# All high products of a chunk's two blocks, then all its low ones, in a two-layer transformer on one core

## The chip, the cores and the metric

The kernel runs on one core of one Trainium2 chip. The metric is the device time of one execution in microseconds; the median of three runs is given. Times of single instructions come from one profiled execution.

## What is computed

Two transformer layers of different kinds follow each other on one sequence of 256 positions with 1024 channels, all in float32. The first joins a gated linear recurrence with a causal attention of 8 heads and a feed-forward part with a causal convolution and GELU; the second joins a windowed attention with a sink and a latent attention, and a SiLU feed-forward part. Most of the work is products of the normed input with weight matrices:

```python
def first_block(x, ...):
    h = rmsnorm(x, norm1_g[l])
    u = jnp.einsum('bsd,de->bse', h, w_in[l])          # recurrence, gates, q, k, v
    ...
    merged = gates0 * (ya @ w_proj_rnn[l]) + gates1 * (yb @ w_proj_attn[l])
    x = x + merged @ w_out[l]
    h = rmsnorm(x, norm2_g[l])
    up = causal_dwconv(h @ w_up[l], ffn_conv_w[l], ffn_conv_b[l])
    x = x + (gelu(up) * (h @ w_gate[l])) @ w_down[l]

def second_block(x, ...):
    proj = rmsnorm_2(x, mix_norm_g[l]) @ w_in[l]
    ...                                                # two attentions of 8 heads
    y = sigmoid(g_a) * (o_a @ w_o_swa[l]) + sigmoid(g_b) * (o_b @ w_o_mla[l])
    x = x + y @ w_out[l]
    h = rmsnorm_2(x, ffn_norm_g[l])
    x = x + (silu(h @ w_gate[l]) * (h @ w_up[l])) @ w_down[l]
    return rmsnorm_2(x, final_norm_g)
```

## The kernel before

The float32 products are made of products in a shorter format (fp32r). A weight chunk of 128 partitions and 2048 columns (1408 in the two down products) comes by one DMA on SP's queue into `wt`; ACT writes its rounded copy `wh`, and DVE the rest, `wl = wt - wh`. Inputs are split in the same way: a tile of `X` holds, for each of two blocks of 128 channels, 256 columns of rounded values and then 256 of the rest. There are three buffers each for `wt`, `wh` and `wl`, and chunks are made two ahead.

A product needs high x high, high x rest and rest x high. For one step k of 128 channels, `group` (L513) issues two matmuls into one PSUM bank of 512 columns. The **high** one takes `wh` as its stationary operand and streams all 512 columns of the input, so that columns 0 to 255 of the bank collect high x high and 256 to 511 collect high x rest. The **low** one takes `wl`, streams the 256 rounded columns and adds into columns 256 to 511. `total` (ACT and DVE) later adds the bank's halves. In `group` high and low of one step stand together: high, low, low, high, low, high and so on.

`mm_T` (L528) makes a chunk of 256 output channels, two blocks b with a bank each, over 8 steps: the first 6 steps of block 0 and of block 1, then the last two of each, since a stage's last input tile may be late. One chunk is 16 highs and 16 lows. It serves `w_x`, `w_g`, the gates, `w_pr`, `w_pa`, `w_out`, `w_up`, `w_gate` and their counterparts of the second layer; `w2_o` uses it in halves of 4 steps. The down products use `group` alone, 11 steps for each chunk (`mm_down` L545, and a loop of its own at the end of the second layer, whose last block goes through `group1` L535, with matmuls of 256 columns only). The projections of the attentions go through `mm_A` (L552), where the weights stream in up to 512 columns and the input is the stationary operand.

What order the instructions stand in is decided by a list scheduler (`Scheduler`). Each instruction has a price in microseconds; the scheduler walks through a modelled time and gives each engine the first instruction in program order that is ready then, or the one that is ready soonest. An instruction waits for those that write what it reads, and for every instruction in `sch.after` at the time it is added. So in the attentions matmuls of `mm_T` stand between the scores, the transposes of the probabilities and the products with the values as fillers. All instructions are issued at L333, which is why every row of the profile has that line.

Of the kernel before, what the change touches and what calls it, by code (L numbers as in the profile page):

```python
# [17 lines left out]
P = 128  # L18
WARM = 4
S = 256  # L20
D = 1024
KD = D // P
# [313 lines left out]
class Engines:  # L336
# [5 lines left out]
    def act(self, out, in_, func, **kw):  # L342
        n = max(out.n, in_.n)
        cost = (0.053 if in_.tile.psum else 0.093) + n / 1200.0
        cost += 0.09 * sum(isinstance(kw.get(k), View) for k in ("scale", "bias")) + (0.1 if "accum_out" in kw else 0.0)
        return self.sch.add("ACT", self.nc.scalar.activation, cost, (out, in_, func), kw, table=SETS.get(func))

    def mm(self, out, a, b, start, stop):
        n = out.n
        if b.dtype == F32R and n >= 256:  # L350
            cost = n / 2400.0 + 0.003
        elif b.dtype == BF16:
            cost = n / 2400.0 + 0.003
        elif n == 1:
            cost = 0.11
        else:
            cost = 4 * n / 2400.0 + 0.006
        self.sch.add("PE", self.nc.tensor.matmul, cost, (out, a, b), dict(start=start, stop=stop, skip_group_check=True))

    def transpose(self, out, in_, idn):  # L360
        self.sch.add("PE", self.nc.tensor.transpose, 2 * out.n / 2400.0 + 0.003, (out, in_, idn), {})
# [28 lines left out]
def build(tc, A, out):  # L390
    from contextlib import ExitStack


    order = []
    _build(None, tc, Scheduler(), A, out, None, order)
    sch = Scheduler()
    with ExitStack() as ctx:
        _build(ctx, tc, sch, A, out, order, [])
        sch.emit(tc)


def _build(ctx, tc, sch, A, out, order, used):
# [19 lines left out]
    mm_ = V.mm  # L422

    def U():
        return up.tile([P, 2, S], F32, tag="u")
# [4 lines left out]
    def T():  # L430
        return tp.tile([P, 2, S], F32, tag="t")
# [10 lines left out]
    def MM():  # L442
        return [B(), B()]
# [29 lines left out]
    def vc(name, i, n=1):  # L473
        return vec[:, VEC[name] + i : VEC[name] + i + n]
# [7 lines left out]
    def produce():  # L482
        i = state["next"]
        name, idx = order[i]
        n = A[name].shape[-1]
        wt = wp.tile([P, 2048], F32, tag="wt")
        wh = wp.tile([P, 2048], F32R, tag="wh")
        wl = wp.tile([P, 2048], F32R, tag="wl")


        cuts = [0, n // 2, n] if i < 4 or i >= fine else [0, n]
        for a, b in zip(cuts, cuts[1:]):
            V.dma("sync", wt[:, a:b], A[name][idx][:, a:b])
            act(wh[:, a:b], wt[:, a:b], AF.Copy)
            V.tensor_sub(wl[:, a:b], wt[:, a:b], wh[:, a:b].bitcast(F32))
        ready[i] = (wh, wl)
        state["next"] = i + 1

    def chunk(name, idx):
        i = len(used)  # L500
        used.append((name, idx))
        if order is None:
            t = wp.tile([P, 2048], F32R, tag="wh")
            return t, t
        assert order[i] == (name, idx)
        while state["next"] <= min(i + LOOK, len(order) - 1):
            produce()
        return ready.pop(i)

    def mv(X, k):  # L510
        return X[k // 2][:, k % 2].rearrange("p h t -> p (h t)")

    def group(ps, W, X, ks, first, last, width, col, xk=0):  # L513

        wh, wl = W
        for k in ks:
            c = slice(k * width + col, k * width + col + P)
            m = mv(X, xk + k)
            hi = lambda st, sp: mm_(ps, wh[:, c], m, start=st, stop=sp)
            lo = lambda: mm_(ps[:, S:], wl[:, c], m[:, :S], start=False, stop=False)  # L520
            if k == first:
                hi(True, False)
                lo()
            else:
                lo()
                hi(False, k == last)

    def mm_T(ps, W, X, kb=KD, k0=0, xk=0):  # L528

        ks = list(range(k0, k0 + kb))  # L530
        for part in (ks[:-2], ks[-2:]):
            for b in range(2):
                group(ps[b], W, X, part, k0, k0 + kb - 1, 256, b * P, xk=xk - k0)

    def group1(ps, W, X, ks, first, last, width, col, xk=0):  # L535

# [29 lines left out]
    def total(ps, dst=None):  # L566

        t = T()
        dst = t if dst is None else dst
        for b in range(2):  # L570
            act(t[:, b], ps[b][:, S:], AF.Copy)
            V.tensor_add(dst[:, b], ps[b][:, :S], t[:, b])
        return dst

    def split(src, X=None):
        X = X or R()
        act(X[:, :, 0], src, AF.Copy)
        V.tensor_sub(X[:, :, 1], src, X[:, :, 0].bitcast(F32))
        return X
# [92 lines left out]
    for k in range(8):  # L672
# [3 lines left out]
        last = V.tensor_sub(w[:, 1], t, w[:, 0].bitcast(F32))  # L676
# [120 lines left out]
    YB = []  # L797
# [50 lines left out]
    def pad():  # L848
        npad[0] += 1
        return pads[npad[0] % 2]  # L850

    YA, HH, XA = [], [], []
# [77 lines left out]
    def gate(name, p, X, later=None):  # L930
        ps = MM()
        mm_T(ps, chunk(name, p), X)
        s = U()
        total(ps, s)
        V.tensor_mul(s, s, rsb)
        if later is None:
            act(s, s, AF.Sigmoid)
        else:
            later.append(s)
        return s  # L940

    M, gates = [], []
    for i in range(6):
        if i < 4:
            gates.append((gate("w_g0", i, X1), gate("w_g1", i, X1)))
        if i < 2:
            continue
        p = i - 2
        g0, g1 = gates[p]
        ps = MM()  # L950
        mm_T(ps, chunk("w_pr", p), YA)
        m0 = total(ps)
        V.tensor_mul(g0, g0, m0)
        ps = MM()
        mm_T(ps, chunk("w_pa", p), YB)
        m1 = total(ps)
        V.tensor_mul(m1, m1, g1)
        V.tensor_add(m1, m1, g0)
        M.append(split(m1))

    def residual(name, X, xin, gname):

        xs, Xs, n = [], [], Norm()
        for p in range(4):
            ps = MM()
            mm_T(ps, chunk(name, p), X)
            y = U()
            for b in range(2):
                V.tensor_add(y[:, b], ps[b][:, :S], xin[p][:, b])
                V.tensor_add(y[:, b], ps[b][:, S:], y[:, b])  # L970
            Xs.append(split_gain(y, gname, p))
            n.add(y)
            xs.append(y)
        return xs, Xs, n

    def down(name, X, xin, rs, gname):
# [12 lines left out]
        return xs, Xs, n  # L989

    x2, X2, n2 = residual("w_out", M, x, "norm2_g")
    rsb = None
    F = []
    for p in range(11):
        ps = MM()
        mm_T(ps, chunk("w_up", p), X2)
        if p == 0:
            rsb, _ = n2.done()
        xr = pad()
        t = total(ps)  # L1000
        V.tensor_mul(xr[:, :, 4:], t, rsb)
        g = T()
        for b in range(2):
            n = 2 * p + b
            act(g[:, b], xr[:, b, 2 : 2 + S], AF.Copy, scale=vc("ffn_conv_w", n))
            for k in range(1, 3):
                V.scalar_tensor_tensor(g[:, b], xr[:, b, 2 + k : 2 + k + S], vc("ffn_conv_w", 22 * k + n), g[:, b], op0=ALU.mult, op1=ALU.add)
            act(g[:, b], g[:, b], AF.Gelu_apprx_tanh, bias=vc("ffn_conv_b", n))
        ps = MM()
        mm_T(ps, chunk("w_gate", p), X2)  # L1010
        t = total(ps)
        V.tensor_mul(t, t, g)
        F.append(split(t))
# [26 lines left out]
    ps = MM()  # L1040
# [19 lines left out]
    ps = MM()  # L1060
# [36 lines left out]
    ps = MM()  # L1097
# [7 lines left out]
    for i in range(2):  # L1105
        pt = B2()
        for hp in range(2):
            for j in range(2):
                c = (2 * i + hp) * P
# [14 lines left out]
    for half in range(2):  # L1124
        ps = MM()
# [38 lines left out]
    for c in range(2):  # L1164
        ps = MM()
# [11 lines left out]
    OS, OM = [], []  # L1177
# [53 lines left out]
    for p in range(4):  # L1231
        W = chunk("w2_o", p)
        ps = MM()
        mm_T(ps, W, OS, kb=4, k0=0)
        m0 = total(ps)
        V.tensor_mul(m0, m0, GA[p])
        ps = MM()
        mm_T(ps, W, OM, kb=4, k0=4)
        m1 = total(ps)
        V.tensor_mul(m1, m1, GB[p])  # L1240
        V.tensor_add(m1, m1, m0)
        Y.append(split(m1))

    x4, X4, n4 = residual("w2_out", Y, x3, "ffn_g")
    F = []
    for p in range(11):
        ps = MM()
        mm_T(ps, chunk("w2_gate", p), X4)
        if p == 0:
            rsb, _ = n4.done()  # L1250
        g = total(ps)
        V.tensor_mul(g, g, rsb)
        silu = act(g, g, AF.Silu)
        V.tensor_mul(g, g, rsb)
        ps = MM()
        mm_T(ps, chunk("w2_up", p), X4)
        t = total(ps)
        V.tensor_mul(t, t, g)
        F.append(split(t))
# [4 lines left out]
    for p in range(4):  # L1264
        y = U()
        ps = MM()
        for b in range(2):
            tail = p == 3 and b == 1
            for j in range(2):
                W = chunk("w2_down", 4 * p + 2 * b + j)  # L1270
# [118 lines left out]
```

## Time and profile before

| | us |
|---|---|
| median of 3 runs | 812.02 |
| lowest, highest | 811.87, 812.77 |
| the profiled execution in all | 812.49 |
| its span, first to last instruction | 810.7 |
| PE busy | 798.5 |
| DVE busy | 603.8 |
| ACT busy | 524.1 |

All busy times are of the profiled execution. In a timeline each line is one instruction, or several of a kind merged, with its start and its duration in us. A matmul begins before the one ahead of it has ended, so durations overlap; what a matmul costs is the distance from its start to that of the next.

### The profile page before, as it was taken

The page shows a single profiled execution, that of the slowest core. Times are in us where ns is not written, and L with a number is a line of the kernel's source. Part 1 is how long each engine was busy: PE and PEld are TensorE (multiplying, and loading weights), DVE is VectorE, ACT ScalarE, POOL GpSimd, SP SyncE. Part 2 cuts the span into 40 slices and gives each one's busy share as a digit, 9 for nine tenths or more (in the row PEclk, how much of TensorE's full clock was granted, in tenths as well). Part 3 has the DMA queues.
Part 4 walks back from the last instruction along what each step waited for, and adds up shares of the span by engine and source line. Part 5 has one row for each costly group of instructions (what it writes and reads, how often), then busy time and mean ns, then how long its engine had stood idle before and what let it go on. Part 6 is the DMA issues. An engine that isn't in the chain of part 4 may idle for free.

```text
span 810.7 us, 11872 instructions
## 1 busy us (share of the span) xinstructions
PE 798.5 (98%) x4520; PEld 689.1 (85%) x4520; DVE 603.8 (74%) x1023; ACT 524.1 (65%) x907; POOL 1.9 (0%) x7
## 2 busy tenths in 40 slices
PE   8999999999999999999999999999999999999996
PEld 6888888888888888888888888888888888888886
DVE  6777869977779788888566776565889877877553
ACT  7979889955455766666445667767656755655451
POOL 0000000000000000000000000000000000000000
PEclk9999999999999999999999999999999999999999
DMA  9742445455555454543556545432456665644541
GB/s 306 308 179 104 163 162 180 158 208 200 171 200 190 174 179 186 207 151 135 193 192 233 187 144 169 144 102 76 134 157 207 204 194 178 204 152 151 179 143 52
DMA packets 32540, 141.05 MB, mean 174 GB/s; under 512 B 3618, under 2 KB 5412, under 8 KB 24420
## 3 DMA queue, kind: packets, MB, share of 16 engines
q1 hardware_dynamic: 32100, 139.41, 50.4%
q0 software_dynamic: 240, 0.79, 0.3%
q8 instruction: 35, 0.57, 0.3%
q14 instruction: 21, 0.17, 0.1%
q10 hardware_dynamic: 144, 0.11, 0.0%
HBM read 139.24 MB, written 1.05 MB: 173 GB/s over the span
## 4 chain that ended last, share of the span: by engine, by line
PE 94%; ACT 2%; DMA 1%; DVE 1%; SPq 0%; issue 0%; DVEq 0%; ACTq 0%
PE b_banks L333 94%; DMA wt_wp<-in_w_q 1%; ACT wh_wp L333 1%; DMA u_up<-in_w_k 1%; ACT t_tp L333 1%; DVE wl_wp L333 0%; SPq L333 0%; DVE u_up L333 0%; DVE t_tp L333 0%; ACT pr_ap L333 0%; DVE pr_ap L333 0%; ACT k_cp L333 0%; DVEq L1384 0%; ACT u_up L333 0%; DVE k_cp L333 0%
## 5 line engine op out<-in xcount | busy, mean ns | idle before, releaser
L333 PE MATMUL b_banks<-r_rp,wh_wp 128*128 128x512 f32 (+1 forms) x1782 | 610.5, 395 | 0.0
L333 PE MATMUL b_banks<-r_rp,wl_wp 128*128 128x256 f32 x1760 | 462.7, 281 | 0.0
L333 PEld LDWEIGHTS b_banks<-r_rp,wh_wp 128*128 128x128 f32 x1782 | 320.6, 188 | 58.8
L333 DVE TENSOR_TENSOR wl_wp<-wt_wp,wh_wp 128x1024 fp32r<-128x1024 f32 (+4 forms) x197 | 299.6, 1537 | 68.2 <-ACT wh_wp L333 67.5
L333 PEld LDWEIGHTS b_banks<-r_rp,wl_wp 128*128 128x128 f32 x1760 | 331.6, 189 | 18.1
L333 ACT ACTIVATE wh_wp<-wt_wp 128x1024 fp32r<-128x1024 f32 (+4 forms) x197 | 253.2, 1308 | 71.0 <-PE b_banks L333 60.3
L333 ACT ACTIVATE t_tp<-b_banks 128x256 f32<-128x256 f32 (+1 forms) x180 | 69.2, 388 | 155.3 <-PE b_banks L333 155.2
L333 DVE TENSOR_TENSOR t_tp<-b_banks,t_tp 128x256 f32<-128x256 f32 (+1 forms) x160 | 61.4, 400 | 42.4 <-ACT t_tp L333 40.7
L333 PE MATMUL b_banks<-wh_wp,r_rp 128*128 128x512 f32 (+2 forms) x296 | 91.9, 388 | 0.0
L333 PEld LDWEIGHTS b_banks<-wh_wp,r_rp 128*128 128x128 f32 x296 | 55.0, 188 | 9.2
L333 PE MATMUL b_banks<-wl_wp,r_rp 128*128 128x512 f32 (+2 forms) x148 | 57.2, 386 | 0.4 <-DVE wl_wp L333 0.2
L333 DVE TENSOR_TENSOR t_tp<-t_tp,u_up 128x512 f32<-128x512 f32 x50 | 34.2, 687 | 2.3 <-ACT t_tp L333 1.5
L333 ACT ACT_TABLE_LOAD x26 | 33.4, 1283 | 1.2 <-PEq L1378 0.7
L333 PEld LDWEIGHTS b_banks<-wl_wp,r_rp 128*128 128x128 f32 x148 | 27.8, 188 | 6.1 <-DVE wl_wp L333 1.6
L333 DVE TENSOR_TENSOR u_up<-b_banks,u_up 128x256 f32<-128x256 f32 x47 | 18.2, 418 | 19.3 <-PE b_banks L333 19.0
L333 DVE TENSOR_TENSOR t_tp<-t_tp,t_tp 128x512 f32<-128x512 f32 (+1 forms) x46 | 25.9, 564 | 5.7 <-ACT t_tp L333 5.3
L333 DVE SCALAR_TENSOR_TENSOR t_tp<-k_cp,k_cp,t_tp 128x256 f32<-128x256 f32 x68 | 28.3, 479 | 0.0
L333 DVE TENSOR_TENSOR r_rp<-t_tp,r_rp 128x512 fp32r<-128x512 f32 x34 | 23.2, 687 | 4.2 <-ACT r_rp L333 3.5
L333 DVE TENSOR_TENSOR u_up<-b_banks,t_tp 128x256 f32<-128x256 f32 x32 | 13.1, 421 | 16.9 <-ACT t_tp L333 16.8
L333 ACT ACTIVATE r_rp<-t_tp 128x512 fp32r<-128x512 f32 x34 | 21.1, 623 | 6.6 <-DVE t_tp L333 6.1
L333 ACT ACTIVATE pr_ap<-pr_ap,s_sp 128x128 f32<-128x128 f32 (+1 forms) x48 | 21.3, 446 | 0.0
L333 ACT ACTIVATE r_rp<-u_up,k_cp 128x256 fp32r<-128x256 f32 x32 | 14.9, 499 | 7.0 <-DVE u_up L333 5.2
(94 smaller groups left out, 467.7 us busy)
## 6 DMA issues: line engine op xcount, KB each, us to landing
wt_wp<-in_w_g SPq DMA_DIRECT2D x12, 1024.0 KB, 4.8
wt_wp<-in_w_up SPq DMA_DIRECT2D x11, 1024.0 KB, 4.7
wt_wp<-in_w_gate SPq DMA_DIRECT2D x11, 1024.0 KB, 4.7
wt_wp<-in_w_down SPq DMA_DIRECT2D x16, 704.0 KB, 4.1
wt_wp<-in_w_gate SPq DMA_DIRECT2D x22, 512.0 KB, 4.8
wt_wp<-in_w_up SPq DMA_DIRECT2D x22, 512.0 KB, 4.1
wt_wp<-in_w_down SPq DMA_DIRECT2D x32, 352.0 KB, 3.1
wt_wp<-in_w_x SPq DMA_DIRECT2D x4, 1024.0 KB, 4.8
```

The source lines that it names most:

```text
L333: op.fn(*[get(a) for a in op.args], **{k: get(v) for k, v in op.kw.items()})
```

## The change

`group` and `mm_T` are rewritten from two helpers, `block_hi` (the highs of one block over some steps) and `block_lo` (its lows). `in_turn` calls such parts one after the other and puts the last instruction of each into `sch.after` for the next, so that the scheduler can't mix them. `mm_T` now issues all highs of block 0, all of block 1, all lows of block 0, all of block 1. The cut ahead of the last two steps remains where the call says `fresh`, at the first chunk of a stage. In the down products one chunk is a row of 11 highs and one of 11 lows. The scheduler's price of an fp32r matmul of n columns goes from n/2400 + 0.003 to (n + 32)/2400 us, that is from 0.216 to 0.227 for a high and from 0.110 to 0.120 for a low, in `mm_A` too.

```diff
     def mm(self, out, a, b, start, stop):
         n = out.n
         if b.dtype == F32R and n >= 256:
-            cost = n / 2400.0 + 0.003
+            cost = (n + 32) / 2400.0
...
+    def block_hi(ps, W, X, ks, first, width, col, xk=0):
+        op = None
+        for k in ks:
+            c = k * width + col
+            op = mm_(ps, W[0][:, c : c + P], mv(X, xk + k), start=k == first, stop=False)
+        return op
+
+    def block_lo(ps, W, X, ks, last, width, col, xk=0):
+        op = None
+        for k in ks:
+            c = k * width + col
+            op = mm_(ps[:, S:], W[1][:, c : c + P], mv(X, xk + k)[:, :S], start=False, stop=k == last)
+        return op
+
+    def in_turn(parts):
+        kept = sch.after
+        for part in parts:
+            op = part()
+            sch.after = kept + (op,)
+        sch.after = kept
+
     def group(ps, W, X, ks, first, last, width, col, xk=0):
...
+        in_turn([
+            lambda: block_hi(ps, W, X, ks, first, width, col, xk),
+            lambda: block_lo(ps, W, X, ks, last, width, col, xk),
+        ])
+
+    def mm_T(ps, W, X, kb=KD, k0=0, xk=0, fresh=False):
         ks = list(range(k0, k0 + kb))
-        for part in (ks[:-2], ks[-2:]):
+        parts = []
+        for run in (ks[:-2], ks[-2:]) if fresh else (ks,):
             for b in range(2):
-                group(ps[b], W, X, part, k0, k0 + kb - 1, 256, b * P, xk=xk - k0)
+                parts.append(lambda run=run, b=b: block_hi(ps[b], W, X, run, k0, 256, b * P, xk - k0))
+            for b in range(2):
+                parts.append(lambda run=run, b=b: block_lo(ps[b], W, X, run, k0 + kb - 1, 256, b * P, xk - k0))
+        in_turn(parts)
...
-        mm_T(ps, chunk("w_pr", p), YA)
+        mm_T(ps, chunk("w_pr", p), YA, fresh=p == 0)
```

How the order moves is shown at three places, all on PE. The first is a chunk of `mm_T` on the normed input near 132 us; `wh` and `wl` are the parts of the weights, `r_rp` the input's tiles, `b_banks` the PSUM banks of the two blocks. Before:

```order
L333 MATMUL b_banks_1691<-r_rp_111,wh_wp_1596 128x512
L333 MATMUL b_banks_1691<-r_rp_111,wl_wp_1619 128x256 x2
L333 MATMUL b_banks_1691<-r_rp_111,wh_wp_1596 128x512
L333 MATMUL b_banks_1691<-r_rp_131,wl_wp_1619 128x256
L333 MATMUL b_banks_1691<-r_rp_131,wh_wp_1596 128x512
L333 MATMUL b_banks_1691<-r_rp_131,wl_wp_1619 128x256
L333 MATMUL b_banks_1691<-r_rp_131,wh_wp_1596 128x512
```

Now:

```order
L333 MATMUL b_banks_1703<-r_rp_111,wh_wp_1575 128x512 x2
L333 MATMUL b_banks_1703<-r_rp_131,wh_wp_1575 128x512 x2
L333 MATMUL b_banks_1703<-r_rp_159,wh_wp_1575 128x512 x2
L333 MATMUL b_banks_1703<-r_rp_187,wh_wp_1575 128x512 x2
L333 MATMUL b_banks_1688<-r_rp_111,wl_wp_1595 128x256 x2
L333 MATMUL b_banks_1688<-r_rp_131,wl_wp_1595 128x256 x2
L333 MATMUL b_banks_1688<-r_rp_159,wl_wp_1595 128x256 x2
```

The alternation of highs and lows has become a row of highs (block 0's eight stand ahead of these eight of block 1) and then a row of lows. In the whole order 61 rows of 16 highs and 30 of 11 stand without anything between, and 136 rows of four or more.

The second place is the opening, where the norm's factors are broadcast (`2x128`, `rows_ap`) and queries and keys are transposed (the rows with `t_tp`), near 26 us. Before:

```order
L333 MATMUL b_banks_309<-wh_wp_223,r_rp_111 128x512 x2
L333 MATMUL b_banks_324<-k_cp_247,k_cp_312 2x128
L333 MATMUL b_banks_309<-wl_wp_232,r_rp_111 128x512
L333 MATMUL b_banks_309<-wh_wp_223,r_rp_131 128x512
L333 MATMUL b_banks_333<-rows_ap_328,k_cp_250 128x128 x2
L333 MATMUL b_banks_309<-wh_wp_223,r_rp_131 128x512
L333 MATMUL b_banks_309<-wl_wp_232,r_rp_131 128x512
L333 MATMUL b_banks_344<-k_cp_247,t_tp_335 128x128
L333 MATMUL b_banks_346<-k_cp_247,t_tp_335 128x128
L333 MATMUL b_banks_309<-wh_wp_223,r_rp_131 128x512 x2
```

Now:

```order
L333 MATMUL b_banks_307<-wh_wp_253,r_rp_187 128x512 x2
L333 MATMUL b_banks_307<-wl_wp_269,r_rp_187 128x512
L333 MATMUL b_banks_351<-k_cp_244,k_cp_331 2x128
L333 MATMUL b_banks_353<-k_cp_244,t_tp_339 128x128
L333 MATMUL b_banks_362<-rows_ap_357,k_cp_248 128x128 x2
L333 MATMUL b_banks_367<-k_cp_244,t_tp_339 128x128
L333 MATMUL b_banks_353<-k_cp_244,t_tp_369 128x128
L333 MATMUL b_banks_353<-k_cp_244,t_tp_339 128x128
```

The broadcast and the first transposes have moved behind the whole query product (bank 307), and the first transposes are those of the queries; `t_tp_369` is ACT's copy of that bank.

The third place is the second attention, where the scores of three heads (`u_up`, two rows each) are followed by transposes of probabilities (`pr_ap`), near 548 us. Before:

```order
L333 MATMUL b_banks_5264<-u_up_4683,u_up_4836 128x256
L333 MATMUL b_banks_5270<-k_cp_247,pr_ap_5259 128x128 x3
L333 MATMUL b_banks_5283<-k_cp_247,pr_ap_5272 128x128
L333 MATMUL b_banks_5285<-r_rp_3743,wh_wp_5035 128x512
L333 MATMUL b_banks_5285<-r_rp_3743,wl_wp_5095 128x256 x2
L333 MATMUL b_banks_5283<-k_cp_247,pr_ap_5272 128x128 x2
```

Now:

```order
L333 MATMUL b_banks_5262<-u_up_4671,u_up_4835 128x256
L333 MATMUL b_banks_5272<-k_cp_244,pr_ap_5266 128x128 x3
L333 MATMUL b_banks_5284<-k_cp_244,pr_ap_5274 128x128 x3
L333 MATMUL b_banks_5291<-r_rp_3755,wh_wp_5015 128x512
L333 MATMUL b_banks_5221<-u_up_4584,ptS_ap_5286 128x64
```

The high and the two lows that stood between the second head's first transpose and its other two are gone from there. On ACT and DVE the order between the engines' own steps moves too, by a few rows at such places; SP's and POOL's rows stand as before.

## Rows read from the trace of the kernel before

**Rows 1.** The page: busy time, share and instructions of PE; the chain by engine.
```profile
PE 798.5 (98%) x4520; PEld 689.1 (85%) x4520; DVE 603.8 (74%) x1023; ACT 524.1 (65%) x907; POOL 1.9 (0%) x7
...
PE 94%; ACT 2%; DMA 1%; DVE 1%; SPq 0%; issue 0%; DVEq 0%; ACTq 0%
```

**Rows 2.** Groups by form, PE: operation, shapes, count, busy us, mean ns, idle.
```profile
L333 PE MATMUL b_banks<-r_rp,wh_wp 128*128 128x512 f32 x1738 | 602.7, 398 | 0.0
L333 PE MATMUL b_banks<-r_rp,wl_wp 128*128 128x256 f32 x1760 | 462.7, 281 | 0.0
```

**Rows 3.** Timeline of PE in `w_down`: start us, duration us, operation, out<-in, count.
```profile
404.38 0.28 PE L333 MATMUL b_banks<-r_rp,wl_wp 128*128 128x256 f32 x1
...
411.10 0.28 PE L333 MATMUL b_banks<-r_rp,wl_wp 128*128 128x256 f32 x1
```

**Rows 4.** Timeline of PE, one chunk of `mm_T`.
```profile
132.50 0.62 PE L333 MATMUL b_banks<-r_rp,wh_wp 128*128 128x512 f32 x2
...
135.55 0.28 PE L333 MATMUL b_banks<-r_rp,wl_wp 128*128 128x256 f32 x1
...
137.98 0.27 PE L333 MATMUL b_banks<-r_rp,wl_wp 128*128 128x256 f32 x1
138.09 0.62 PE L333 MATMUL b_banks<-r_rp,wh_wp 128*128 128x512 f32 x2
```

**Rows 5.** Timeline of PE in `w2_o`: two highs, two lows, next high.
```profile
573.22 0.62 PE L333 MATMUL b_banks<-r_rp,wh_wp 128*128 128x512 f32 x2
573.69 0.40 PE L333 MATMUL b_banks<-r_rp,wl_wp 128*128 128x256 f32 x2
573.92 0.40 PE L333 MATMUL b_banks<-r_rp,wh_wp 128*128 128x512 f32 x1
```

**Rows 6.** Timeline of PE, 512 columns only, in an attention projection.
```profile
77.07 0.39 PE L333 MATMUL b_banks<-wl_wp,r_rp 128*128 128x512 f32 x1
...
79.15 0.39 PE L333 MATMUL b_banks<-wl_wp,r_rp 128*128 128x512 f32 x1
...
86.63 0.39 PE L333 MATMUL b_banks<-wl_wp,r_rp 128*128 128x512 f32 x1
```

**Rows 7.** Timeline of PE, 256 columns only, at the end of `w2_down`.
```profile
794.00 0.28 PE L333 MATMUL b_banks<-r_rp,wl_wp 128*128 128x256 f32 x1
...
801.57 0.28 PE L333 MATMUL b_banks<-r_rp,wl_wp 128*128 128x256 f32 x1
```

**Rows 8.** Timeline of ACT in the opening, the steps named in the change.
```profile
24.24 0.60 ACT L333 ACTIVATE t_tp<-b_banks 128x512 f32<-128x512 f32 x1
...
24.88 0.28 ACT L333 ACTIVATE k_cp<-b_banks 128x128 f32<-128x128 f32 x1
...
25.28 0.49 ACT L333 ACTIVATE k_cp<-k_cp,k_cp 128x4 f32<-128x4 f32 x2
25.95 0.27 ACT L333 ACTIVATE rows_ap<-b_banks 2x128 f32<-2x128 f32 x1 [0.18 <-PE b_banks L333]
```

**Rows 9.** Stages: window, us, busy of engines (instructions), granted clock, DMA share, GB/s.
```profile
35.00:131.00 96.00, 95.69 (x499) 81.29 (x497) 74.08 (x151) 83.41 (x170) 1.74 (x3) 1.00 0.44 154
...
497.00:569.00 72.00, 69.53 (x457) 60.14 (x456) 44.44 (x150) 51.73 (x133) 0.00 (x0) 1.00 0.35 115
```

**Rows 10.** Timeline of DVE: the last tile of `F`.
```profile
383.82 0.68 DVE L333 TENSOR_TENSOR r_rp<-t_tp,r_rp 128x512 fp32r<-128x512 f32 x1
```

**Rows 11.** Timeline of PE, second attention; idle time before, and its releaser, in brackets.
```profile
549.79 0.71 PE L333 MATMUL b_banks<-k_cp,pr_ap 128*128 128x128 f32 x3 [1.11 <-ACT pr_ap L333]
550.26 0.48 PE L333 MATMUL b_banks<-r_rp,wh_wp 128*128 128x512 f32 x1
550.58 0.40 PE L333 MATMUL b_banks<-r_rp,wl_wp 128*128 128x256 f32 x2
550.81 0.38 PE L333 MATMUL b_banks<-k_cp,pr_ap 128*128 128x128 f32 x2
```

**Rows 12.** The page: weight loads of the lows, count, busy us, mean ns.
```profile
L333 PEld LDWEIGHTS b_banks<-r_rp,wl_wp 128*128 128x128 f32 x1760 | 331.6, 189 | 18.1
```

More of the change, by code (lines that the diff above doesn't have):

```diff
@@ L357, in mm @@
             cost = 4 * n / 2400.0 + 0.006
-        self.sch.add("PE", self.nc.tensor.matmul, cost, (out, a, b), dict(start=start, stop=stop, skip_group_check=True))
+        return self.sch.add("PE", self.nc.tensor.matmul, cost, (out, a, b), dict(start=start, stop=stop, skip_group_check=True))
     def transpose(self, out, in_, idn):
@@ L511, in mv @@
         return X[k // 2][:, k % 2].rearrange("p h t -> p (h t)")
-    def group(ps, W, X, ks, first, last, width, col, xk=0):
[L515 to L528, printed above, removed]
+    def block_hi(ps, W, X, ks, first, width, col, xk=0):
[16 more added lines that the diff above has]
+        sch.after = kept
+    def group(ps, W, X, ks, first, last, width, col, xk=0):
+        in_turn([
[3 more added lines that the diff above has]
+    def mm_T(ps, W, X, kb=KD, k0=0, xk=0, fresh=False):
         ks = list(range(k0, k0 + kb))
-        for part in (ks[:-2], ks[-2:]):
+        parts = []
+        for run in (ks[:-2], ks[-2:]) if fresh else (ks,):
             for b in range(2):
-                group(ps[b], W, X, part, k0, k0 + kb - 1, 256, b * P, xk=xk - k0)
+                parts.append(lambda run=run, b=b: block_hi(ps[b], W, X, run, k0, 256, b * P, xk - k0))
+            for b in range(2):
+                parts.append(lambda run=run, b=b: block_lo(ps[b], W, X, run, k0 + kb - 1, 256, b * P, xk - k0))
+        in_turn(parts)
     def group1(ps, W, X, ks, first, last, width, col, xk=0):
@@ L954, in _build @@
         ps = MM()
-        mm_T(ps, chunk("w_pa", p), YB)
+        mm_T(ps, chunk("w_pa", p), YB, fresh=p == 0)
         m1 = total(ps)
@@ L965, in residual @@
             ps = MM()
-            mm_T(ps, chunk(name, p), X)
+            mm_T(ps, chunk(name, p), X, fresh=p == 0)
             y = U()
@@ L995, in _build @@
         ps = MM()
-        mm_T(ps, chunk("w_up", p), X2)
+        mm_T(ps, chunk("w_up", p), X2, fresh=p == 0)
         if p == 0:
@@ L1009, in _build @@
         ps = MM()
-        mm_T(ps, chunk("w_gate", p), X2)
+        mm_T(ps, chunk("w_gate", p), X2, fresh=p == 0)
         t = total(ps)
@@ L1233, in _build @@
         ps = MM()
-        mm_T(ps, W, OS, kb=4, k0=0)
+        mm_T(ps, W, OS, kb=4, k0=0, fresh=p == 0)
         m0 = total(ps)
@@ L1237, in _build @@
         ps = MM()
-        mm_T(ps, W, OM, kb=4, k0=4)
+        mm_T(ps, W, OM, kb=4, k0=4, fresh=p == 0)
         m1 = total(ps)
@@ L1247, in _build @@
         ps = MM()
-        mm_T(ps, chunk("w2_gate", p), X4)
+        mm_T(ps, chunk("w2_gate", p), X4, fresh=p == 0)
         if p == 0:
@@ L1255, in _build @@
         ps = MM()
-        mm_T(ps, chunk("w2_up", p), X4)
+        mm_T(ps, chunk("w2_up", p), X4, fresh=p == 0)
         t = total(ps)
```

## Prediction

> **What bounds the kernel now.** I read the page first, its shares by engine and its chain. PE is busy for 98% of the span and carries 94% of the chain that ended last [rows 1], so the time is PE's, and idle time of the other engines costs nothing until PE waits for it. Next came the groups of instructions by form, which say what PE does: 1738 high matmuls of 512 columns and 1760 low ones of 256 [rows 2], of which 22 stand in the unchanged end of `w2_down`. The mean of one, 398 and 281 ns, is a duration with its overlap and no pitch. So from the timeline of PE I took starts, and divided the distance of two of them by the matmuls between. In `w_down`, 404.38 to 411.10 us, 19 pairs of low and high take 6.72 us, 0.3537 a pair [rows 3]. A chunk of `mm_T`, from the last high ahead of it at 132.50 to its own last at 138.09, takes 5.59 us for 16 pairs, 0.3494 each; its last stretch, seven pairs from 135.55 to 137.98, takes 0.347 [rows 4]. So alternation runs at two speeds, 0.354 and 0.347, and a chunk of `mm_T` mixes them. No engine releases PE in these stretches, and the granted clock is 1.00 in the stages shown, its 2.4 GHz level [rows 9].
>
> **What equal matmuls cost.** Two places of this trace have long rows of one width, each with a weight load of its own. In a projection of the attention, 33 matmuls of 512 columns from 79.15 to 86.63 us take 7.48, 0.2267 each [rows 6]; there the weights stream and the input is loaded, but the widths are those of a high. At the end of `w2_down`, 63 of 256 columns from 794.00 to 801.57 take 7.57, 0.1202 each [rows 7]. A pair at these pitches costs 0.3469.
>
> **The change, part by part.** *Rows in place of pairs.* No matmul is added or removed. In the order, the 61 rows of 16 highs that nothing cuts and the 30 rows of 11 in the down products show that the rows stand. `mm_T` has 88 chunks' worth of 16 pairs (84 of 16 and 8 halves of 8 in `w2_o`): 5.59 - 16 x 0.3469 = 0.040 us each, 3.5 us. The down products have 330 pairs: 0.3537 - 0.3469 = 0.0068 each, 2.2 us. Together 5.7 us, if a row were at its pitch at once.
>
> *Settling.* It isn't always. After an interruption, the nine matmuls from 77.07 to 79.15 take 2.08 us where 9 x 0.2267 is 2.04, a loss of 0.04 [rows 6]. The nearest row to the change's own crossing is better: in `w2_o` two highs and two lows in turn, begun right behind two lows, take 0.70 us (573.22 to 573.92) where two uniform pairs take 0.694 [rows 5]. The order has 136 rows of four or more highs. At 0.01 each they lose 1.4 us, at 0.04 5.4 us, at best nothing. I take 0.01, since that row crosses from lows to highs as the new order does. Crossing to lows costs nothing in it: two lows take 0.23.
>
> *Weights and inputs.* The high row needs all `wh` of a chunk within 16 x 0.227 = 3.6 us, the lows need `wl` only then; before, both were needed at once, so the later of the two, DVE's, gets 3.6 us of slack, and `wh` is freed sooner. SP's and POOL's queues keep their order, row for row. Of the inputs, the last tile of `F` is needed earlier: before, 11 + 9 pairs after the start of `w_down` at about 380.4, so 7.0 us; now 11 pairs and 9 highs, 5.9 us, at 386.3. DVE ends that tile at 384.5 [rows 10], so 1.8 us of cover remain, and nothing is charged. At a stage's first chunk `fresh` keeps the last two k for the end, where they were. The new bindings order PE's own instructions against each other only; a wait on `wl` now holds the row behind it, which has the 3.6 us.
>
> *The corrected price of a matmul.* The scheduler took 0.326 us for a pair and now takes 0.347, so PE passes fewer matmuls before an instruction that comes back from ACT and DVE, and stalls move. Two places in the order show it. (a) In the opening, the broadcast of the norm and the transposes of queries and keys now stand behind the whole second query product, and ACT's copy of the second query block behind four smaller steps. These take 0.27, 0.49 and 0.40 (start to start), and the copy 0.60 [rows 8]: 1.76 us. PE meanwhile has two transposes and four short matmuls at about 0.11 and the wait for the first of the steps, 0.27, in all 0.93. The price is 0.8 us; before, PE stood between these without a wait that long, and at best the value is 0. (b) In the second attention PE is idle 2.47 of 72 us [rows 9]. Where three heads' scores are followed by transposes, PE waited 1.11 us at 549.79 for the first head's probabilities, and the second head's last two transposes came at 550.81 [rows 11]. Before, one high and two lows lay between, 0.47 us; now all six transposes stand together. I charge 0.5 us, with bounds of 0 and 1.0. The first attention has 0.31 us of idle time in 96 [rows 9], so it can only lose, 0 to 1.0 us; I take 0, as its fillers keep their places.
>
> **Sum.** 5.7 - 1.4 - 0.8 - 0.5 = 3.0 us. Of the profiled execution, 812.49 us in all with a span of 810.7, that leaves a span of about 807.7 and 809.5 us in all; its own time is 0.5 above the median of the runs, 812.02, and from the median the forecast is **809.0 us**.
>
> A rule of the Trainium skill speaks against this. "TensorE: Matmul & The Clock Gate", section "Back-to-back issue gap", gives a warm gap of N / 2.4 + 2.5 ns, with nothing for the neighbour; by it a pair would take 0.325 us in either order and the rows would gain nothing. The trace differs in both points: its settled pitches are 0.2267 and 0.1202, and alternation costs 0.347 or 0.354 by its history.
>
> **Rivals.** *The order makes no difference.* What slows alternation would then be a cost of the load and matmul in themselves, and rows would run at 0.350 a pair as well. For it: alternation already runs at 0.347 in part. Against it: the rows at 0.2267 and 0.1202 hold for 7.5 us without one exception. It gives the median plus none or all of the stalls above, 812.0 to 813.3.
>
> *Lows bound by their loads.* A load has a mean duration of 189 ns [rows 12] and a low only 0.12 us to hide it. If loads ran one behind the other, each low in a row would take 0.189, and 1738 x 0.069 = 120 us would be lost. The 63 matmuls of [rows 7] each have their load and pass at 0.1202; I give it no chance.
>
> *Slower, by settling and stalls.* Rows that lose 0.04 each give back 5.4 of the 5.7 us; with stalls of 0.8, 1.0 and 1.0 the sum is 812.0 - 0.3 + 2.8 = 814.5. With the stalls at their upper ends the sign turns when a row loses 0.021 us or more. For it: PE's idle time in the attentions is small now, and the better price takes away slack. Against it: the crossing in [rows 5] loses 0.01.
>
> *All free.* No settling and no new stall: 812.0 - 5.7 = 806.3.
>
> That the rows do not come about is excluded by the order.
>
> **How the numbers follow.** The forecast has 0.70, no difference 0.14, slower 0.10, all free 0.06. Within 0.2% (1.6 us, about what a measurement of this kernel can tell from no change) means 810.4 to 813.6. The forecast's case reaches above 810.4 with some 0.04 of its 0.70, where a row loses about 0.02. So faster 0.66 + 0.06 = 0.72, same 0.14 + 0.04 = 0.18, slower 0.10. The range begins at all free, 806.3, a little lower for rounded pitches, 806.0, and ends at 812.8, which takes in half of the no-difference case and leaves out the slower one: some 0.17 to 0.2.
>
> **What would show it.** Right: in a row of 16 highs the starts lie 0.227 apart after at most three matmuls, lows 0.120; a chunk of `mm_T` takes 5.55 to 5.56 us where it took 5.59, and one of `w_down` 11 x 0.347 = 3.82 where it took 3.89; PE's idle time grows by about 1.3 us, in the opening before the query transposes and where six transposes follow three heads' scores. Wrong: starts in the highs' rows that keep to 0.230 to 0.236; lows over 0.125; a wait of PE for `wh` at a chunk's start or for `F` at about 9 highs into the second row of the down product; idle time in the first attention.

## The result: slower, and where the profile puts it

The changed kernel takes 818.44 us (817.06 to 822.64) where the kernel before takes 812.08 in the same runs: a ratio of 1.0081, with a 95% interval of 1.0060 to 1.0101. The forecast was 809.0, so not only the size but the sign was wrong. The profiled execution has a span of 816.7 us and took 818.43 in all.

The page of the changed kernel, parts 1 and 4, answers to [rows 1]:

```profile
PE 798.1 (98%) x4520; PEld 693.1 (85%) x4520; DVE 593.8 (73%) x1023; ACT 519.6 (64%) x907; POOL 1.9 (0%) x7
...
PE 86%; DVE 6%; ACT 3%; DMA 2%; issue 1%; SPq 0%; DVEq 0%; ACTq 0%
```

PE's busy time is about what it was, and the rest of its span, its idle time, has gone from 12.2 to 18.6 us. PE's share of the chain that ended last has gone from 94% to 86%, and DVE has 6% of it. The starts show the two sides: the rows pass faster, and the time was lost in waits.

**The rows.** PE's timeline of the changed kernel, first in `w_gate` and `w_up`, then in `w_down` (answers to [rows 3, 4]):

```profile
293.12 3.82 PE L333 MATMUL b_banks<-r_rp,wh_wp 128*128 128x512 f32 x16
296.78 2.08 PE L333 MATMUL b_banks<-r_rp,wl_wp 128*128 128x256 f32 x16
298.69 3.82 PE L333 MATMUL b_banks<-r_rp,wh_wp 128*128 128x512 f32 x16
...
382.19 2.68 PE L333 MATMUL b_banks<-r_rp,wh_wp 128*128 128x512 f32 x11
384.71 1.48 PE L333 MATMUL b_banks<-r_rp,wl_wp 128*128 128x256 f32 x11
386.02 3.72 PE L333 MATMUL b_banks<-r_rp,wh_wp 128*128 128x512 f32 x15
```

By starts, a chunk of `mm_T` takes 298.69 - 293.12 = 5.57 us (before 5.59, forecast 5.55 to 5.56), one of `w_down` 386.02 - 382.19 = 3.83 (before 3.89, forecast 3.82). To see all of it, I took every distance between two starts on PE, subtracted the settled pitch of its form (0.2267 for 512 columns, 0.1200 for 256 and so on), and called what stands in one place and is over 0.1 us a wait, the remainder unsteady pitch. The two sums, worked out so for each kernel's profiled execution, are used from here on: before, 12.1 us of waits and 7.1 of unsteady pitch; after, 20.4 and 3.7. The rows gave 3.4 us, and the waits took 8.3.

**The waits.** What PE waited for, in total, times, and the longest, first before, then after:

```profile
PE b_banks L333 <- ACT pr_ap L333: 2.0, 4, 1.1
...
PE b_banks L333 <- DVE t_tp L333: 0.3, 1, 0.3
```

```profile
PE b_banks L333 <- ACT pr_ap L333: 3.9, 7, 0.8
PE b_banks L333 <- DVE t_tp L333: 2.2, 3, 1.1
PE b_banks L333 <- ACT rows_ap L333: 1.4, 1, 1.4
PE b_banks L333 <- DVE r_rp L333: 1.3, 1, 1.3
```

By place, the new waits are 1.2 us in the opening (17 to 32 us), 1.7 in the first attention with its recurrence (most of it 1.37 at 124.29), 3.5 in the second attention (500 to 554; the largest 2.50 at 517.39, where the kernel before waited 0.99), 1.6 at 603.59, the first chunk of `w2_out`, and the rest scattered. None is a wait for a weight's DMA on PE's side, and none is at a chunk's `wh` in the long stages.

**One such wait in its rows.** The recurrence's product at 125.71 waits for DVE's convolution. The changed kernel, PE, ACT and DVE:

```profile
115.89 1.80 PE L333 MATMUL b_banks<-r_rp,wl_wp 128*128 128x256 f32 x13
117.53 1.48 PE L333 MATMUL b_banks<-u_up,u_up 128*128 128x128 f32 x8
...
125.71 1.10 PE L333 MATMUL b_banks<-t_tp,r_rp 128*128 128x256 f32 x4 [1.14 <-DVE t_tp L333]
```

```profile
115.83 1.95 ACT L333 ACTIVATE wh_wp<-wt_wp 128x2048 fp32r<-128x2048 f32 x1
```

```profile
117.81 2.29 DVE L333 TENSOR_TENSOR wl_wp<-wt_wp,wh_wp 128x2048 fp32r<-128x2048 f32 x1 [1.11 <-ACT wh_wp L333]
120.02 0.68 DVE L333 TENSOR_TENSOR r_rp<-b_banks,r_rp 128x512 fp32r<-128x512 f32 x1
...
121.28 0.34 DVE L333 CUSTOM_DVE_ANT_0 pr_ap<-b_banks,k_cp,k_cp 128x128 f32<-128x128 f32 x1
...
123.42 2.53 DVE L333 SCALAR_TENSOR_TENSOR t_tp<-k_cp,k_cp,t_tp 128x256 f32<-128x256 f32 x6
```

ACT begins a weight cast (the 19th of the kernel's 197) at 115.83, while 13 lows of a chunk whose highs ended at 114.2 still stand ahead of PE. DVE's half of the cast follows at 117.81, 0.3 us after the scores have begun, and holds DVE for 2.2 us. The softmax's first step, which needs the scores, starts at 121.28, 3.75 us after their first product, and the convolution ends at 125.9. The chain that ended last goes the same way, from the cast over DVE to PE (start us, us, what):

```profile
115.97 1.81 ACT wh_wp L333
117.81 2.29 DVE wl_wp L333
123.50 2.07 DVE t_tp L333 x5
125.71 374.12 PE b_banks L333 x2117
```

The kernel before at the same place, with the same cast:

```profile
116.50 1.47 PE L333 MATMUL b_banks<-u_up,u_up 128*128 128x128 f32 x8
```

```profile
123.29 1.91 ACT L333 ACTIVATE wh_wp<-wt_wp 128x2048 fp32r<-128x2048 f32 x1
```

```profile
117.36 0.35 DVE L333 CUSTOM_DVE_ANT_0 pr_ap<-b_banks,k_cp,k_cp 128x128 f32<-128x128 f32 x1 [0.61 <-PE b_banks L333]
```

There the cast begins 6.8 us after the scores, behind the attention's small steps, where now it begins 1.7 us ahead of them, and the softmax's first step stands 0.86 us behind the scores. This reading led to the theory of the second set of runs, below.

### The profile page after: what moved, and what is told of

Same layout as the page of the kernel before. It is cut to its first block, busy times and chain, and to the rows that moved or that the text cites. A ratio compares the mean times of both kernels' runs of the same rounds, so it can differ in the third digit from the quotient of the medians.

```text
span 816.7 us, 11900 instructions
## 1 busy us (share of the span) xinstructions
PE 798.1 (98%) x4520; PEld 693.1 (85%) x4520; DVE 593.8 (73%) x1023; ACT 519.6 (64%) x907; POOL 1.9 (0%) x7
## 4 chain that ended last, share of the span: by engine, by line
PE 86%; DVE 6%; ACT 3%; DMA 2%; issue 1%; SPq 0%; DVEq 0%; ACTq 0%
PE b_banks L333 86%; DVE t_tp L333 3%; DVE wl_wp L333 2%; DMA wt_wp<-in_w_v 1%; ACT wh_wp L333 1%; DVE u_up L333 1%; DMA wt_wp<-in_w_q 1%; ACT t_tp L333 1%; DVE pr_ap L333 1%; DMA u_up<-in_x 1%; ACT pr_ap L333 0%; ACT L333 0%; SPq L333 0%; DVE r_rp L333 0%; DVE k_cp L333 0%
## 5 line engine op out<-in xcount | busy, mean ns | idle before, releaser
L333 PE MATMUL b_banks<-r_rp,wh_wp 128*128 128x512 f32 (+1 forms) x1782 | 440.7, 392 | 1.3 <-DVE r_rp L333 1.3
L333 PEld LDWEIGHTS b_banks<-r_rp,wl_wp 128*128 128x128 f32 x1760 | 230.4, 191 | 10.2
L333 PE MATMUL b_banks<-r_rp,wl_wp 128*128 128x256 f32 x1760 | 237.4, 283 | 0.0
L333 ACT ACTIVATE t_tp<-b_banks 128x256 f32<-128x256 f32 (+1 forms) x180 | 62.4, 376 | 2.4 <-PE b_banks L333 1.8
L333 DVE TENSOR_TENSOR t_tp<-b_banks,t_tp 128x256 f32<-128x256 f32 (+1 forms) x160 | 58.8, 395 | 3.7 <-ACT t_tp L333 3.3
L333 DVE TENSOR_TENSOR t_tp<-t_tp,u_up 128x512 f32<-128x512 f32 x50 | 34.2, 687 | 15.1 <-ACT t_tp L333 12.5
L333 ACT ACTIVATE t_tp<-t_tp,k_cp 128x256 f32<-128x256 f32 x38 | 17.5, 503 | 11.2 <-DVE t_tp L333 11.2
L333 ACT ACTIVATE t_tp<-u_up 128x512 f32<-128x512 f32 (+2 forms) x21 | 11.4, 541 | 18.2 <-DVE u_up L333 18.2
```

The lines of the kernel that those rows point to most:

```text
L333: op.fn(*[get(a) for a in op.args], **{k: get(v) for k, v in op.kw.items()})
```

## The experiments

All times are medians, and ratios are against the kernel before on the same chip, whose median lay between 812.5 and 812.7 us.

**First set: price, rows or bindings.** I first took the corrected price for the cause, since it was the part whose stalls I had charged.

e1, the changed kernel with the old price:

```diff
-            cost = (n + 32) / 2400.0
+            cost = n / 2400.0 + 0.003
```

> Rows and bindings as in the changed kernel, but the scheduler's price of a matmul is the old one, n/2400 + 0.003. Comparing the starts on PE, the changed kernel saves 3.4 us by steadier pitches and loses 8.3 us by waits. Theory 'price': the old price was too low by 0.021 us a pair, so everything that PE waits for stood later than it needed to, a built-in reserve, and the corrected price spent it. Then the waits fall back to about those of the kernel before and the time is 812.1 - 3.4 = 808.7 us. Rival 'rows': the waits come from the rows and bindings themselves (inputs wanted earlier, coarser fillers). Then it stays at 816 to 819 us. Rival 'lottery': any new order moves the waits by some us either way, and the time lies anywhere from 809 to 819 without a pattern.

Measured: 819.4 us, ratio 1.0093 (1.0069 to 1.0116). The theory "price" falls: the loss is all there without it. In the profiled execution the waits at 17 to 30 us are back to those of before, but the waits at 123.09 us (1.62 us long), 515.63 (2.50), 550.00 (2.47), 597.69 (0.93) and 602.82 (1.60) are there.

e2, the kernel before with only the price corrected (the same line, the other way):

> The kernel before with one line changed: the price is (n + 32)/2400, highs and lows still alternate. Theory 'price': the reserve is gone here too, and the time rises by most of the 8.3 us of new waits, to 817 to 820 us, with the waits on ACT's and DVE's steps in the opening and the attentions grown. Rival 'rows': nothing but small moves, 811 to 814 us.

Measured: 814.13 us, ratio 1.0021 (1.0011 to 1.0031), between the two expectations: the price by itself costs 1.4 to 1.7 us. 0.7 of it is in the opening, where the wait at the norm's broadcast and the transposes is 0.56 + 0.50 us and was 0.21 + 0.20.

e3, rows in the down products alone, at the old price; `mm_T` calls `pairs`, a copy of the old `group`:

```diff
-        in_turn(parts)
+        for part in (ks[:-2], ks[-2:]):
+            for b in range(2):
+                pairs(ps[b], W, X, part, k0, k0 + kb - 1, 256, b * P, xk=xk - k0)
```

> Rows only in the two down products, where no other stage depends on the fillers; mm_T alternates as before, and the price is the old one. All theories: the down products give back up to 330 x 0.0068 = 2.2 us, less about 0.3 for the settling of 30 rows, and no new waits elsewhere, so 810.0 to 810.6 us. If the time doesn't fall, the rows' gain in the trace of the changed kernel was no gain of the rows.

Measured: 811.43 us, ratio 0.9987 (0.9979 to 0.9996). Faster, by 1.3 of the 2.2 us, and above the expected range; unsteady pitch is 5.6 us, 1.5 less than before. The gain of the rows is real, and these stages lose nothing by them.

e4, the changed kernel without the bindings:

```diff
             op = part()
-            sch.after = kept + (op,)
```

> The changed kernel without the bindings: highs and lows are still written in rows and the price is the new one, but in_turn no longer puts the last instruction of a part into sch.after, so the scheduler may pull a low or the next block forward while a high waits. Theory 'price': the waits stay, 816 to 819 us. Rival 'rows': if it is the bindings that hold PE behind a late input, the waits at 517 and 603 us in the changed kernel shrink and the time is 810 to 814 us.

Measured: 817.4 us, ratio 1.0055 (1.0042 to 1.0068), in the range of "price", which e1 rules out. The wait at 603 is gone, the one at 517 isn't. So the bindings are a small part, and the rows themselves, bound or not, make most of the waits.

The profiled executions of the four and the two kernels, in us, worked out as above:

| | waits | unsteady pitch | median |
|---|---|---|---|
| before | 12.1 | 7.1 | 812.5 |
| changed | 20.4 | 3.7 | 818.4 |
| e1, old price | 19.7 | 3.4 | 819.4 |
| e2, price alone | 14.5 | 7.2 | 814.1 |
| e3, rows in down alone | 12.5 | 5.6 | 811.4 |
| e4, unbound | 24.4 | 3.5 | 817.4 |

(e4's waits can't be compared with the others: its profiled execution took 821.3 us, and in two stretches, one of them below, the granted clock is at 0.50, the 1.2 GHz level, so that slow matmuls count as waits there. Its other five executions took 816.5 to 818.6.)

```profile
522.00:526.00 4.00, 4.00 (x17) 3.42 (x17) 0.99 (x4) 1.17 (x4) 0.00 (x0) 0.50 0.78 256
```

**Second set: why rows make waits.** The rows at 115 us gave the new theory. With alternation a chunk's last high and last low stand side by side, and its `wh` and `wl` buffers come free together. In rows `wh` is done with 2 us earlier, and more where attention work stands between. The scheduler gives ACT the next cast at once, since its place in the program is ahead of the attention's steps; DVE's half of the cast follows, and each is one instruction of about 2 us (1.95 on ACT, 2.29 on DVE in the rows above), so that the engine's next step stands behind the whole of it.

e5 is e1 with the early release taken back; `held` keeps each chunk's `wl`, whose readers are the lows:

```diff
+            sch.after = kept + tuple(o for _, _, o in held[i - 3].tile.readers) if i - 3 in held else kept
             act(wh[:, a:b], wt[:, a:b], AF.Copy)
+            sch.after = kept
```

> Rows, bindings and the old price as in e1, with one thing put back: ACT's cast of a chunk into a wh buffer also waits for the last low product of the chunk that used the buffer's number three chunks ago, so wh comes free together with wl, as it did when highs and lows alternated. Theory 'early casts': in e1 the highs of a chunk are over 2 to 3 us before its lows, so the scheduler casts the next weights earlier, ACT 1.9 us and DVE 2.2 us, right ahead of steps that PE waits for; in e1 the recurrence's wait at 123 us (1.6 us), the wait at 515 us (2.5 against 1.0) and those at 504, 529 and 550 us (2.0 more together) come from it. They fall back, the waits at 597 and 602 us (2.5 us) stay, and the time is 819.4 - 5.1 = 814.3, between 812.5 and 815.5 us. Rival 'granularity': the waits come from longer fillers on PE, and the time stays at 817 to 820 us.

Measured: 811.11 us, ratio 0.9979 (0.9970 to 0.9988); 1.4 below the range, and from e1 8.3 us less, 3 more than the waits of e1's profiled execution had let expect (e7 shows where these probably come from). The waits at 123, 504 and 515 are those of the kernel before (none, 0.20, 0.99). The rows of e5 at the place shown above, ACT and DVE:

```profile
117.19 1.92 ACT L333 ACTIVATE wh_wp<-wt_wp 128x2048 fp32r<-128x2048 f32 x1
```

```profile
117.34 0.35 DVE L333 CUSTOM_DVE_ANT_0 pr_ap<-b_banks,k_cp,k_cp 128x128 f32<-128x128 f32 x1 [0.32 <-PE b_banks L333]
...
119.63 2.29 DVE L333 TENSOR_TENSOR wl_wp<-wt_wp,wh_wp 128x2048 fp32r<-128x2048 f32 x1
```

On ACT the cast now begins 0.7 us after the scores (116.48) and not 1.7 ahead of them, and on DVE it comes behind the softmax's first steps, which stand 0.86 us after the scores again. PE, in rows as in e1, goes on without a wait, so the rival, that long rows are poor fillers, falls.

e6, e5 and no bindings (the line of e4):

> As e5, and in_turn no longer puts the last instruction of a part into sch.after. Theory: at the start of w2_out PE runs out of work while the last input tiles are on their way, since in each of three chunks only four highs of the first block may go and the second block is bound behind the first; without the binding the second block's four may go too. The waits at 597 and 602 us go, 2.5 us less than e5, and with the 3.4 us that steadier pitches give, the time is 811.8, between 809.0 and 812.5 us, about as far below the kernel before as rows alone are worth less their crossings. Rival: the bindings cost nothing, and the time is that of e5.

Measured: 808.64 us, ratio 0.9950 (0.9938 to 0.9963). This version is faster than both kernels, and below its range's lower end by 0.4. It has 13.4 us of waits and 2.9 of unsteady pitch. At the start of `w2_out` PE's timeline of the changed kernel:

```profile
600.54 1.59 PE L333 MATMUL b_banks<-r_rp,wl_wp 128*128 128x256 f32 x12
601.97 2.00 PE L333 MATMUL b_banks<-r_rp,wh_wp 128*128 128x512 f32 x8
605.31 1.20 PE L333 MATMUL b_banks<-r_rp,wh_wp 128*128 128x512 f32 x4 [1.33 <-DVE r_rp L333]
```

and of e6:

```profile
596.35 1.60 PE L333 MATMUL b_banks<-r_rp,wl_wp 128*128 128x256 f32 x12
597.78 4.04 PE L333 MATMUL b_banks<-r_rp,wh_wp 128*128 128x512 f32 x17
601.66 0.64 PE L333 MATMUL b_banks<-r_rp,wl_wp 128*128 128x256 f32 x4
```

While the last input tile is on its way through `total`, the products and the split, PE needs other work. Bound, the following chunks can give only highs of their first block, and after 8 of them PE waits 1.33 us for the tile. Without the binding their second blocks give some too: 13 of the 17 highs are of later chunks, the last 4 those that need the tile, and no wait is left.

e7, e1 without the bindings, with the early release:

> e1 without the bindings and without the later release: rows and the old price. Theory: the waits at 597 and 602 us go, those from the early casts stay, 819.4 - 2.5 = 816.9, between 815.5 and 818 us. If the bindings are harmless it stays at 819.4; if they are the main cause it falls to 811 or less.

Measured: 819.13 us, ratio 1.0082 (1.0068 to 1.0095). The waits at 597 and 602 are gone as expected, but the time is what "harmless" had forecast. The granted clock tells why the 2.5 us don't show. Rows by stretch of e1, then of e7 (busy us of PE, PEld, DVE, ACT, POOL with instructions; granted clock; DMA share; GB/s):

```profile
514.00:518.00 4.00, 2.49 (x18) 1.72 (x18) 3.40 (x11) 1.91 (x7) 0.00 (x0) 1.00 0.00 2
518.00:522.00 4.00, 3.67 (x26) 3.06 (x26) 3.41 (x16) 3.09 (x12) 0.00 (x0) 1.00 0.12 16
...
556.00:562.00 6.00, 6.00 (x41) 5.33 (x40) 1.12 (x3) 2.89 (x5) 0.00 (x0) 1.00 0.29 113
```

```profile
514.00:518.00 4.00, 2.48 (x16) 1.55 (x15) 3.78 (x13) 1.98 (x8) 0.00 (x0) 0.92 0.01 4
518.00:522.00 4.00, 3.92 (x16) 3.27 (x15) 2.44 (x12) 2.54 (x11) 0.00 (x0) 0.50 0.16 35
...
556.00:562.00 6.00, 6.00 (x26) 5.46 (x26) 1.06 (x4) 1.73 (x6) 0.00 (x0) 0.52 0.55 175
562.00:566.00 4.00, 4.00 (x26) 3.50 (x25) 0.69 (x1) 1.26 (x3) 0.00 (x0) 1.00 0.00 0
```

Both executions wait about 2.5 us around 516 us. In e7 the clock then falls to 0.50, its 1.2 GHz level, and PE passes 16 matmuls in the next 4 us where it passed 26. The loss at that place, waits and slow matmuls together, is 5.26 us in e7 and 2.50 in e1, so the fall costs 2.8 us; the second, at 552 us, 3.0. It does not happen in every execution: the six of e1 have mean clocks from 0.998 (816.66 us) to 0.988 (823.78), the four of e7 all 0.988 to 0.990. At like mean clocks e7 is the faster: e1's two executions at 0.988 took 822.64 and 823.78 us, e7's four 818.59 to 820.89. So e7 saved the binding's 2.5 us or a little more and lost as much to the clock. e1's profiled execution had no such fall; its median, at a mean clock of 0.994, fits one, though no execution with one fall was profiled.

**Third set: the price again, and another way to hold `wh`.**

e8, e6 with the corrected price:

> e6 (rows, wh released late, no bindings) with the corrected price (n + 32)/2400. What the price costs by itself, where no casts come early. If the price costs what it cost the alternating kernel in e2 (1.4 us, most of it in the opening, where ACT's small steps stand behind a query copy and a cast), the time is 808.6 + 1.4 = 810.0, between 809.2 and 811.5 us. If the price is right and harms only in company with early casts, 808.0 to 808.9 us.

Measured: 812.05 us, ratio 0.9993 (0.9984 to 1.0002): the price costs 3.4 us there, more than expected. Leaving out the first 22 us, whose waits for the first loads differ from execution to execution, its profiled execution has 2.4 us more of waits than that of e6: 0.6 in the opening, 0.4 in the first attention, 0.5 at 463 and 1.0 between 499 and 506, and 0.2 less after that. The other 1.0 us I can't place; it is no more than single executions differ by, as e8's profiled one took 1.0 us less than its median and e6's 1.0 more.

e9, the changed kernel itself with the later release as its one addition:

> The changed kernel itself (rows, bindings, corrected price) with the one addition that ACT's cast into a wh buffer waits for the last low product that used the buffer's number before. Theory 'early casts': this alone takes away most of the loss, 818.4 - 8.3 (what e5 took from e1) = 810.1, plus the price's 1.4 at most: 810 to 812.5 us. Rival: with the corrected price the release matters less, and the time stays above 815 us.

Measured: 812.79 us, ratio 1.0006 (0.9997 to 1.0015), 0.3 above the first range. From 1.0081 this takes back 0.75%, 6.1 us, and leaves the kernel where the one before is.

e10, rows in the other order, with nothing added to the casts (`mm_T` of e1, where `head` is the first high of each block, issued ahead of this; `group` in the same way):

```diff
+            head = [k for k in run if k == k0]
...
             for b in range(2):
                 parts.append(lambda run=run, b=b: block_lo(ps[b], W, X, run, k0 + kb - 1, 256, b * P, xk - k0))
+            for b in range(2):
+                parts.append(lambda run=run[len(head) :], b=b: block_hi(ps[b], W, X, run, k0, 256, b * P, xk - k0, k0 + kb - 1))
```

> Another way to keep wh in use to a chunk's end, without any added wait on the casts: e1 with the rows in the other order, the first high of each block (which starts the bank), then all lows, then the other highs. Now wl comes free first and wh last, so the next cast by ACT can't begin before the chunk's end and DVE's follows it. Theory 'early casts': the time is that of e5 less or more some crossings, 810 to 813 us, and the waits at 123 and 515 us are back at nothing and 1.0 us. Rival, that the row form itself (long stretches without a change of operand) makes the waits: 817 to 820 us.

Measured: 813.99 us, ratio 1.0016 (1.0007 to 1.0025), 1 us above the range but 5.4 below e1. No wait is left at 123 us. At 514 DVE takes the softmax ahead of the cast, as in the kernel before; 2.04 us of waits stand there all the same, the first 0.39 long as before, a later one of 0.84 new. That one is for the copy of the transposed probabilities, and this copy stands right behind half a cast on ACT:

```profile
515.35 1.04 ACT L333 ACTIVATE wh_wp<-wt_wp 128x1024 fp32r<-128x1024 f32 x1
516.29 0.47 ACT L333 ACTIVATE ptS_ap<-b_banks 128x384 f32<-128x384 f32 x1
```

e13, e10 without the bindings:

> e10 (lows ahead of the highs, nothing added to the casts) without the bindings. In e10 the casts stand behind the attention's steps again, and what is left over the kernel before is in the waits at the start of w2_out (594 to 601 us, 2.1 us) and in the second attention (1.0 at 515 us). Theory: the bindings make both, and the time is that of e6 plus the crossings of the two leading highs, 809 to 811.5 us. Rival: lows first costs by itself, since the lows need wl at once, and the time stays at 813 to 815 us.

Measured: 808.93 us, ratio 0.9956 (0.9942 to 0.9969), just below the range and level with e6. At 514 the wait is 0.99 again. So two ways to hold `wh` that share nothing but the time at which it comes free, a dependency in e6 and another order of the rows here, give the same gain. In all, the four kernels with `mm_T` in rows and early casts (the changed one, e1, e4, e7) took 817.4 to 819.4 us, and the seven that hold `wh` 808.6 to 814.0, so the rival "lottery" of e1 falls for the casts.

e11, e6 with a price below the old one:

```diff
-            cost = n / 2400.0 + 0.003
+            cost = n / 2400.0 - 0.008
```

> e6 (rows, wh released late, no bindings, price n/2400 + 0.003) with the price 0.011 lower still, n/2400 - 0.008. The corrected price cost 3.4 us in e8. Theory 'reserve': what PE waits for is scheduled later than it need be when a matmul is priced too low, so a price below the old one lengthens the reserve and takes away more waits: 806.8 to 808.4 us. Rival 'lottery': the price only reshuffles the order, and any price other than the old one costs: 809.5 to 812.5 us.

Measured: 808.79 us, ratio 0.9959 (0.9947 to 0.9972), the same as e6 and between the two ranges. Whether the corrected price costs because it takes away a reserve, or because it only reshuffles the order, stays open: more reserve gains nothing, but no loss came either.

## Why the prediction was wrong, step by step

From kernel to kernel the medians run 812.5 (before), 808.6 (rows, nothing bound, `wh` held to the chunk's end, e6), 811.1 (bindings added, e5), 819.4 (early release added, e1), and 818.4 with the corrected price, the changed kernel: -3.9, +2.5, +8.3 and -1.0. The last two steps mix with the clock's falls, which e1's median seems to contain. The profiled executions of e1 and of the changed kernel, both at a granted clock of 1.00 from 10 to 800 us, took 816.66 and 818.43 us, so by them the corrected price costs 1.8 us here too and is no gain, and the changed kernel's loss is there without a fall.

**Rows and settling: right.** The forecast was 5.7 - 1.4 = 4.3 us. Unsteady pitch fell by 3.4 us in the changed kernel and by 4.2 in e6, and e6 as a whole gained 3.9. Single rows settled later than I said, after five or six highs and not three: by starts, one row of `w_gate` begins with 0.234, 0.236, 0.228, 0.232, 0.231 before it holds 0.227. That loses 0.03 a row, and the first low behind it takes 0.113 instead of 0.120, so that 0.007 comes back; 0.02 net is twice the 0.01 I took from [rows 5]. The lows run at 0.120 as forecast, and the rivals "no difference" and "bound by their loads" are both gone. By the isolated gap of the Trainium skill ("TensorE: Matmul & The Clock Gate", "Back-to-back issue gap") neither order would matter. Here the settled pitch stays at 0.2267 and 0.1200, and the order was worth 3.4 to 4.2 us.

**"`wh` is freed sooner": the step that failed.** The prediction named it under weights and inputs, as slack, and gave it no cost. I saw that SP's and POOL's queues kept their order, noted of ACT's and DVE's only that a few rows move, and did not ask which: the casts moved ahead of the attention's steps. This is worth 8.3 us between e1 and e5 and 6.1 between the changed kernel and e9. The undisturbed part is the 5 us of waits that e1 has over e5 (19.7 against 14.8); the rest fits one fall of the clock, 2.8 us, in most executions of e1.

**"The new bindings order PE's own instructions against each other only": wrong.** They also bar work that could have filled a wait for an input, 1.6 us at 603 us in the changed kernel and 2.5 us between e5 and e6. I had asked whether the last two k were needed earlier and not what PE had to do meanwhile.

**The corrected price: right in kind, somewhat low in size.** I had charged 1.3 us; it cost 1.4 in e2, 1.7 from e5 to e9 and 3.4 in e8. The opening's 0.8 us has the right place: the opening has 1.2 us more of waits in the changed kernel and 0.7 in e2. But what PE waits 1.41 us for is a step behind another cast, which itself waited for its load; ACT in the changed kernel:

```profile
28.57 1.91 ACT L333 ACTIVATE wh_wp<-wt_wp 128x2048 fp32r<-128x2048 f32 x1 [1.16 <-DMA wt_wp<-in_w_v]
30.39 0.25 ACT L333 ACTIVATE rows_ap<-b_banks 2x128 f32<-2x128 f32 x1
```

The second attention's 0.5 came out at 3.5 and the first attention's 0 at 1.7, both beyond my bounds, but mainly by the casts: in e5, at the old price, 0.4 and 0 are left of them, and in e9, at the corrected one, about 1.0 and 0.5.

**The rival "slower, by settling and stalls"** had the right sign at 814.5, for the wrong reason: its price was a row's loss of 0.04 and stalls of the price correction. No rival had the casts.

## What to carry to other kernels

When a change lets a buffer go earlier, look up which work waits for that buffer, on which engine it will now start, and what it stands in front of; here casts of 2 us, each one instruction, pulled ahead of chains of small steps, cost more than the rows gained. In an order made by a scheduler, compare the orders of all engines at the latency-bound places, not only the queue that the edit is about. Binding work into rows takes fillers away: bind only where the rows are worth more than the freedom, and hold buffers until the point at which their refilling does no harm.

## What the runs showed of the hardware

A wait of about 2.5 us on PE is followed in some executions, not in all, by a stretch at the 1.2 GHz level that costs another 2.8 to 3.0 us (e7 at 518 and 556 us), so a new wait can cost twice what the timeline shows, and the single times of a kernel with such waits scatter: 816.7 to 823.8 us in e1, against 808.3 to 809.6 in e6. The Trainium skill ("TensorE: Matmul & The Clock Gate", "What's actually happening") says that the slow clock is the default and activity lifts it. The rows agree as far as they go: in e7 the clock fell behind the wait and was at 1.00 again from 562 us on, after PE had been busy without a gap from 556. That one execution pays where another doesn't is shown by e1 and e7 at the same wait, and within one kernel by e4, whose executions at mean clocks of 0.993 to 0.997 took 816.5 to 818.6 us and the one at 0.988 took 821.3. What decides it stays open. A granted clock between the two levels need not mean slow matmuls: e11's profiled execution shows 0.95 from 20 to 800 us, and its highs and lows keep the 0.227 and 0.120 that they have at 1.00. And a row of equal matmuls passes its first five or six more slowly, 0.228 to 0.236 against 0.227 us, nearly every time it follows narrower ones.
